# The closing of an expert layer: the residual of all groups but the last beside the last products, two norms together, and gathers paced in two parts

## The chip, the cores and the metric

The kernel runs on one core of one Trainium2 chip. The metric is the device time of one execution in microseconds, the median of the runs shown. The engines are named as in the profile: PE is TensorE (its matrix products, with PEld the loading of weights), DVE is VectorE, ACT is ScalarE, POOL is GpSimd, SP is SyncE, whose queue issues most of the transfers. A line such as L1323 is a line of the kernel before.

## The reference

One layer over 1024 latent tokens of width 1024 (and 256 context tokens): a mixer (a Mamba-2 head group and a convolution group, one output projection), then a retrieval layer over 16384 single-neuron experts, then a norm. The change touches only the retrieval layer's end and its order:

```
s = einsum(q, sub_keys); sv, si = top_k(s, 16)              # per token, 8 heads, two halves of the key
best, flat = top_k(sv0[:, None] + sv1[None, :], 16)         # the choice: 8 x 16 = 128 experts a token
experts, gates = i1 * 128 + i2, softmax(best)
act = gelu(einsum("pd,ped->pe", x, u_tab[experts]))
y   = einsum("pe,ped->pd", gates * act, v_tab[experts])
x   = x + mod5 * y
return rms_norm(x, final_norm_w)                            # x * rsqrt(mean(x*x) + eps) * w
```

## The kernel before

**Two ways to the same sum.** The 1024 tokens are eight blocks of 128. The first ND = 5 blocks are computed densely: the 16384 experts are cut into 128 tiles, called experts here, of 128 neurons; for each of them PE multiplies all 640 tokens by the tile's u (In), ACT takes the Gelu, DVE weighs it with a matrix of gates that is zero where a token has not chosen the neuron, and PE multiplies the result by the tile's v (Out). The other three blocks are gathered: for each token and each of its 128 choices one row of u and later one row of v is fetched by an indirect transfer of POOL (128 rows of 1024 numbers, one to a partition), and one instruction of DVE uses it: L1311 multiplies with the token and sums (a u step), L1323 multiplies by the weight and adds to `ac` (a v step). A block has 128 u steps and 128 v steps, so there are 768 row steps.

**Products in three.** Every fp32 product is made as three in a reduced format, of high and low parts. ACT makes the high part (`hi_lo`, L60; L984 for u; L1412 for the weighed activations), DVE the low one by a subtraction (L61, L988, L1416). So each In and Out needs an instruction of ACT and then one of DVE before PE can multiply.

**The order of the expert loop** is written out by hand. GE = 8 experts are a group, and there are 16 groups. `seq` holds 8 Ins, then for each group 8 Outs of the first half of the columns (512), one In of the next group, 8 Outs of the second half, 7 Ins. In one item: begin the splits, loads and gates that are due some items ahead; weigh the In before; the item's products (`mm`); then `advance`; then the low half of the In before, and the Gelu. The five PSUM tiles `pv` (one a block) collect the 8 Outs of a half, and `Out.sum` (L1457) adds them to `acc`, which is a part of h2T, after each half of each group. The last half of the last group is not run in the loop: its eight Outs are `closing`.

**advance** is what puts other work beside the products. An In calls it with (2, 18), an Out with (1, 11): so many pieces of the last choice (block 7's top-k on DVE, with parts on POOL; 100 pieces in all), and so many units on `units[0]`. For the units, it runs steps of the generator `gathered()`: one row step each, 768 of them, and ten more with which the last block is closed (`finish`, L1258 to L1274: its residual, its norm and its output). Experts 0 to 2 call no advance. While the choice runs there are NGB = 5 buffers for gathered rows; when it has ended, its memory is freed and NMORE = 2 more are opened. What is left of the steps after the loop runs in one go.

**The end before.** In the last eight Outs of the loop the memory of the Ins is given back (at the second of them, `far == 1`), and rw (the gate row, broadcast), final_norm_w and the five x1 tiles are loaded through SP's queue; the splits of the closing Outs are begun two more ahead with every Out, up to all eight. Behind the loop, block by block: `Close.mm` multiplies the block's 24 closing products into a PSUM tile `pf` (three buffers); `residual(0)` computes acc * rw + x1 on the first 512 columns of the next block, and ACT its squares' sum; `post` adds pf to the second 512 columns, does their residual, sums the squares, takes the inverse root (`rsqrt`, L95 to L101, small instructions of DVE around one Sqrt of ACT), scales the 1024 columns (L1494) and issues the block's output.

Of the kernel before, what the change touches and what calls it, by code (L numbers as in the profile page):

```python
# [8 lines left out]
F32 = mybir.dt.float32  # L9
# [4 lines left out]
AF = mybir.ActivationFunctionType  # L14
OP = mybir.AluOpType
# [3 lines left out]
P = 128  # L19
D = 1024  # L20
KD = D // P
T = 1024
NT = T // P
# [10 lines left out]
NEXP = 16384  # L34
# [3 lines left out]
ND = 5  # L38
# [2 lines left out]
NS = 7  # L41
NGB, NMORE = 5, 2
IN_US, OUT_US = 18, 11
NU, NV = 3, 3
GE = 8

# [26 lines left out]
def layer_kernel(ctx, tc, A, dbg=None):  # L73
    nc = tc.nc
# [98 lines left out]
    with ExitStack() as st:  # L173
# [12 lines left out]
        for j in range(8):  # L186
# [5 lines left out]
            c = (j + 4) % 8 * 256  # L192
# [179 lines left out]
    with ExitStack() as st:  # L372
# [126 lines left out]
        for n, c in enumerate(order):  # L499
# [13 lines left out]
            elif c >= 16 and c < 20:  # L513
                i = c - 16
# [262 lines left out]
    with ExitStack() as st:  # L777
# [63 lines left out]
        def residual(z, half, x1, p):  # L841
            cs = slice(half * 512, half * 512 + 512)
            nc.vector.tensor_tensor(x1[:, cs], p, gater[:, cs], op=OP.mult)
            nc.vector.tensor_tensor(x1[:, cs], x1[:, cs], B[z][0][:, cs], op=OP.add)
# [399 lines left out]
    with ExitStack() as st:  # L1244
# [85 lines left out]
        more, self_end = [], object()  # L1330
        steps = gathered()
        next(steps)
        units = [0, 0]

        SE = {}

# [20 lines left out]
        def advance(n, us):  # L1357

            for _ in range(n):
                if not more and next(choice, self_end) is self_end:  # L1360

                    last_choice.close()
                    more.append(st.enter_context(tc.tile_pool(name="more", bufs=NMORE, reuse_waits="tile")))
            units[0] += us
            while units[1] * (NEXP // P * (IN_US + 2 * OUT_US) - 3 * IN_US) < units[0] * ((NT - ND) * 2 * P + 20):
                next(steps, None)
                units[1] += 1

        W = {}
        NG = NEXP // P // GE  # L1370
# [47 lines left out]
        class Out:  # L1418
# [28 lines left out]
                advance(1, OUT_US)  # L1447

            def sum(self):
                if self.i < GE - 1:  # L1450
                    return
                for t in range(ND):
                    a = acc[:, t, self.cs]
                    if self.g == 0:
                        nc.scalar.activation(a, Out.pv[t], AF.Copy)
                    else:
                        nc.vector.tensor_tensor(a, a, Out.pv[t], op=OP.add)  # L1457
# [4 lines left out]
        class Close:  # L1462
# [6 lines left out]
                self.x = tail.tile([P, D], F32, name="x1", bufs=ND)  # L1469
                nc.sync.dma_start(self.x, x1_dram[self.t * P:(self.t + 1) * P, :])  # L1470

            def residual(self, half):
                cs = slice(half * 512, half * 512 + 512)
                a = self.a[:, cs]
                nc.vector.tensor_tensor(a, a, rw[:, cs], op=OP.mult)
                nc.vector.tensor_tensor(a, a, self.x[:, cs], op=OP.add)
                nc.scalar.activation(self.x[:, cs], a, AF.Square, accum_out=sf[:, self.t, half:half + 1])

            def mm(self, outs):
                self.pv = psF.tile([P, 512], F32, name="pf")  # L1480
# [3 lines left out]
                    for j, (x, y) in enumerate(((wl, o.vh), (wh, o.vl), (wh, o.vh))):  # L1484
                        nc.tensor.matmul(self.pv, x[:, sl], y, start=o.i == 0 and j == 0, stop=o.i == GE - 1 and j == 2)

            def post(self):
                t, a = self.t, self.a
                nc.vector.tensor_tensor(a[:, 512:], a[:, 512:], self.pv, op=OP.add)
                self.residual(1)  # L1490
                s2, r = sf[:, t, 2:3], sf[:, t, 3:4]
                nc.vector.tensor_tensor(s2, sf[:, t, 0:1], sf[:, t, 1:2], op=OP.add)
                rsqrt(r, s2, 1.0 / D, 1)
                nc.vector.scalar_tensor_tensor(a, a, r, spare_w, op0=OP.mult, op1=OP.mult)  # L1494
                nc.sync.dma_start(A["out"][t * P:(t + 1) * P, :], a)

        seq = [In(i) for i in range(GE)]
        for g in range(NG):
# [29 lines left out]
        for n, x in enumerate(seq[:-GE]):  # L1528
            far = 0
            if len(seq) - n <= 2 * GE:  # L1530
                far = x.i
                if far == 1:

                    late.close()
                    tail = late.enter_context(tc.tile_pool(name="tail", bufs=GE, side="right", reuse_waits="tile"))
                    psF = late.enter_context(tc.tile_pool(name="psF", bufs=3, space=PSUM, side="right", reuse_waits="tile"))
                    rw = tail.tile([P, D], F32, name="rw", bufs=1)
                    nc.sync.dma_start(rw, row_dram[0].partition_broadcast(P))
                    nc.sync.dma_start(spare_w, A["final_norm_w"].partition_broadcast(P))
                    sf = tail.tile([P, ND, 4], F32, name="sf", bufs=1)  # L1540
                    ends = [Close(t) for t in range(ND)]
                    for c in ends:
                        c.load()
            begin(In, "split", 2)
            begin(Out, "split", 2 + far)
            begin(Out, "load", NV + 2 + far)
            before = seq[n - 1] if n and isinstance(seq[n - 1], In) else None
            if before:
                before.weigh()
            passed[type(x)] += 1  # L1550
            begin(In, "gate", 2)
            begin(In, "lower", 1)
            begin(In, "load", NU + 1)
            x.mm()
            if before:
                before.low()
            x.post()
        for _ in steps:
            pass
        dbg("idx", idx)  # L1560
        dbg("gates", gates)
        begin(Out, "split", GE)
        ends[0].residual(0)
        for c in ends:
            c.mm(closing)
            if c.t + 1 < ND:
                ends[c.t + 1].residual(0)
            c.post()
    late.close()
    sel.close()  # L1570

# [59 lines left out]
```

## Time and profile before

| | |
|---|---|
| median of 3 runs | 3053.84 us (3052.66 to 3054.78) |
| the profiled execution: time, span | 3052.06 us, 3050.3 us |
| PE busy | 2836.3 us, 93% |
| DVE busy | 2570.6 us, 84% |
| ACT busy | 1060.9 us, 35% |
| POOL busy | 1326.0 us, 43% |
| mean granted clock of PE | 0.968 |

The span runs from the first to the last instruction; the time of the execution holds 1.8 us more around it. The busy shares are means over stages that differ: a stage is judged by what waits in it. A wait stands in brackets behind an instruction as the idle time of its engine before it, and what ended it.

### The profile page before, as it was taken

To read this page: it belongs to the slowest core of one execution; us is meant where nothing else is said; L and a number is where in the kernel's file an instruction comes from. 1 tells how busy PE (TensorE), PEld (TensorE's weight loads), DVE (VectorE), ACT (ScalarE), POOL (GpSimd) and SP (SyncE) were. 2 spreads that over 40 slices of the span, in tenths; PEclk is the share of its full clock that TensorE was granted. 3 is DMA by queue.
4 is the path that set the end of the run, shared out by engine and by line. 5 is a ranking of instruction groups with operands and counts; after the bars stand their busy time and mean duration, and the time that the engine had idled before them with its cause. 6 is when DMAs were issued, how large, how long until landed. Compare 5 with 4: busy or idle time off the path is not lost.

```text
span 3050.3 us, 41960 instructions
## 1 busy us (share of the span) xinstructions
PE 2836.3 (93%) x15129; PEld 2391.2 (78%) x15129; DVE 2570.6 (84%) x5084; ACT 1060.9 (35%) x2026; POOL 1326.0 (43%) x1043
## 2 busy tenths in 40 slices
PE   7999899998888876999999999999999999999996
PEld 3777698764555556898888998998998898998995
DVE  4898756659999999889989998888998888888886
ACT  3224333333667664332222222222222322322222
POOL 0212343420000002666566656566666566666650
PEclk8999899999999987999999999999999999999998
DMA  6211256250221235888889999998998998999993
GB/s 214 61 36 42 86 165 213 77 189 15 118 107 63 111 125 192 308 312 301 311 297 361 324 346 343 326 340 320 337 344 317 334 357 318 336 342 318 328 326 119
DMA packets 334545, 722.68 MB, mean 237 GB/s; under 512 B 24560, under 2 KB 167168, under 8 KB 333056
## 3 DMA queue, kind: packets, MB, share of 16 engines
q0 software_dynamic: 112176, 408.47, 37.1%
q1 hardware_dynamic: 222160, 311.53, 29.5%
q8 instruction: 119, 1.95, 0.2%
q14 instruction: 90, 0.74, 0.1%
HBM read 658.56 MB, written 61.35 MB: 236 GB/s over the span
## 4 chain that ended last, share of the span: by engine, by line
PE 58%; DVE 27%; issue 5%; DMA 5%; POOL 3%; ACT 2%; SPq 0%; DVEq 0%; POOLq 0%; ACTq 0%
PE pa L996 22%; PE pv L1444 8%; PE pv L1445 8%; PE pv L1443 8%; PE pa L68 4%; DVE o L1219 3%; DVE cfm L413 2%; DVE oh L1091 2%; DVE ob L1211 2%; POOL gr L1286 2%; DVE oh L1089 2%; DVE gr L1311 1%; DVE ef L1077 1%; PE pq L953 1%; PE po L68 1%
## 5 line engine op out<-in xcount | busy, mean ns | idle before, releaser
L1286 POOL DMA_INDIRECT gr<-in_peer_v_dram,idx x384 | 546.8, 1424 | 309.3 <-DVE h2T L1323 209.7
L1286 POOL DMA_INDIRECT gr<-in_peer_u_dram,idx x384 | 524.1, 1365 | 361.4 <-DVE gr L1311 249.2
L1444 PE MATMUL pv<-vl,wh 128*128 128x512 f32 x1240 | 495.5, 400 | 19.5 <-DVE vl L61 17.3
L1323 DVE SCALAR_TENSOR_TENSOR h2T<-gr,wv,h2T 128x1024 f32<-128x1024 f32 x381 | 488.5, 1282 | 13.6 <-DMA gr<-in_peer_v_dram,idx 6.0
L1443 PE MATMUL pv<-vh,wl 128*128 128x512 f32 x1240 | 493.4, 398 | 1.5 <-ACT vh L60 1.4
L1445 PE MATMUL pv<-vh,wh 128*128 128x512 f32 x1240 | 493.6, 398 | 0.0
L1311 DVE SCALAR_TENSOR_TENSOR gr<-gr,h2T 128x1024 f32<-128x1024 f32 x384 | 455.5, 1220 | 23.5 <-DMA gr<-in_peer_u_dram,idx 23.3
L60 ACT ACTIVATE vh<-v 128x512 fp32r<-128x512 f32 x256 | 161.5, 632 | 656.1 <-PE pv L1445 616.7
L996 PE MATMUL pa<-hh,ul 128*128 128x320 f32 x2000 | 335.0, 310 | 3.2 <-DVE ul L988 3.2
L996 PE MATMUL pa<-hh,uh 128*128 128x320 f32 x2000 | 334.6, 309 | 0.0
L996 PE MATMUL pa<-hl,uh 128*128 128x320 f32 x2000 | 334.0, 309 | 0.3 <-ACT ga L1406 0.3
L996 PEld LDWEIGHTS pa<-hl,uh 128*128 128x128 f32 x2000 | 304.8, 188 | 3.3 <-ACT ga L1406 0.6
L996 PEld LDWEIGHTS pa<-hh,ul 128*128 128x128 f32 x2000 | 304.2, 188 | 3.7 <-DVE ul L988 3.7
L996 PEld LDWEIGHTS pa<-hh,uh 128*128 128x128 f32 x2000 | 304.4, 188 | 0.0
L1444 PEld LDWEIGHTS pv<-vl,wh 128*128 128x128 f32 x1240 | 235.0, 190 | 80.0 <-DVE vl L61 22.8
L1406 ACT ACTIVATE ga<-pa 128x320 f32<-128x320 f32 x252 | 109.2, 436 | 525.2 <-PE pa L996 507.1
L1443 PEld LDWEIGHTS pv<-vh,wl 128*128 128x128 f32 x1240 | 235.1, 190 | 57.8 <-ACT vh L60 2.4
L61 DVE TENSOR_TENSOR vl<-v,vh 128x512 fp32r<-128x512 f32 x256 | 176.4, 690 | 122.5 <-ACT vh L60 114.9
L1445 PEld LDWEIGHTS pv<-vh,wh 128*128 128x128 f32 x1240 | 235.3, 190 | 56.1
L1197 PEld LDWEIGHTS pg<-o,o 128*128 128x128 f32 x1280 | 174.1, 207 | 128.2 <-ACT o L1214 109.2
L1197 PE MATMUL pg<-o,o 128*128 128x128 f32 x1280 | 188.0, 297 | 75.7 <-ACT o L1214 67.3
L1214 ACT ACTIVATE o<-ob,tr 128x128 f32<-128x128 bf16 x640 | 209.4, 399 | 96.4 <-DVE ob L1211 94.4
(344 smaller groups left out, 4241.5 us busy)
## 6 DMA issues: line engine op xcount, KB each, us to landing
v<-in_peer_v_dram SPq DMA_DIRECT2D x256, 256.0 KB
u<-in_peer_ut_dram SPq DMA_DIRECT2D x87, 512.0 KB
g_dram<-stg SPq DMA_DIRECT2D x10, 4096.0 KB
gm<-g_dram SPq DMA_DIRECT2D x64, 640.0 KB
h2T<-in_peer_ut_dram SPq DMA_DIRECT2D x41, 512.0 KB
ld<-in_ada_w_dram SPq DMA_DIRECT2D x24, 512.0 KB
w<-in_w_in_t_dram SPq DMA_DIRECT2D x21, 512.0 KB
raw<-in_ada_w_dram SPq DMA_DIRECT2D x8, 1024.0 KB
```

The lines of the kernel that those rows point to most:

```text
L60: nc.scalar.activation(hi, src, AF.Copy)
L61: (eng or nc.vector).tensor_tensor(lo, src, hi.bitcast(F32), op=OP.subtract)
L68: nc.tensor.matmul(out, a(k)[i], b(k)[j], start=start and t == 0 and k == 0, stop=stop and t == 2 and k == n - 1)
L996: nc.tensor.matmul(pa[half], x[:, k], y[:, k, half * TH:half * TH + TH], start=t == 0 and k == 0, stop=t == 2 and k == KD - 1)
L1197: nc.tensor.matmul(pg[:, j], o2[:, j], o1[:, j], start=True, stop=True)
L1214: nc.scalar.activation(o2[:, j], ob[:, :, j], AF.Copy, scale=tr[:, 1, t4 * 4 + j:t4 * 4 + j + 1])
L1286: nc.gpsimd.indirect_dma_start(out=g, out_offset=None, in_=A[t], in_offset=bass.IndirectOffsetOnAxis(ap=idx[:, b, e:e + 1], axis=0))
L1311: nc.vector.scalar_tensor_tensor(g, g, 1.0, h2, op0=OP.mult, op1=OP.mult, accum_out=act[:, e:e + 1])
L1323: nc.vector.scalar_tensor_tensor(ac, g, wv[:, e:e + 1], ac, op0=OP.mult, op1=OP.add)
L1443: nc.tensor.matmul(Out.pv[t], wl[:, sl], self.vh, start=i == 0, stop=False)
L1444: nc.tensor.matmul(Out.pv[t], wh[:, sl], self.vl, start=False, stop=False)
L1445: nc.tensor.matmul(Out.pv[t], wh[:, sl], self.vh, start=False, stop=i == GE - 1)
```

## The change

- `advance` runs its steps at two paces. Until the choice is done, a unit is worth 0.85 x 782 / 4918 steps (before: 788 / 5066); from then on, what is left of 782 is spread over what is left to unit 4918, that is LEAD = 60 units before the loop's end at unit 4978. So all steps, the closing of the last block too, are issued within the loop.
- `Out.sum` is left out for the last group. In the last Outs of the loop (from `far == 4` on, one block each) and behind the loop (block 4), `residual` computes a * rw + x1 on all 1024 columns, of the sums of all groups but the last.
- Behind the loop, `add(0, pv)` for the five blocks: x = pv * rw, a += x, and ACT the squares' sum, on the first half; the second half likewise from pf after each block's closing products.
- `norm` takes the inverse roots of blocks 0 and 1 together, and 2 and 3; then `post` scales. Block 3 is scaled after block 4's add, block 4 alone, in two halves with an output each.

```diff
+LEAD = 60
@@ advance
-            units[0] += us
-            while units[1] * (NEXP // P * (IN_US + 2 * OUT_US) - 3 * IN_US) < units[0] * ((NT - ND) * 2 * P + 20):
+            end, num = NEXP // P * (IN_US + 2 * OUT_US) - 3 * IN_US - GE * OUT_US - LEAD, (NT - ND) * 2 * P + 14
+            units[1] += us * (0.85 * num / end if not more else (num - units[2]) / max(end - units[0], us))
+            units[0] += us
+            while units[2] < min(units[1], num):
                 next(steps, None)
-                units[1] += 1
+                units[2] += 1
@@ Out.sum
-                if self.i < GE - 1:
+                if self.i < GE - 1 or self.g == NG - 1:
                     return
@@ Close
-            def residual(self, half):
+            def residual(self):
+                nc.vector.tensor_tensor(self.a, self.a, rw, op=OP.mult)
+                nc.vector.tensor_tensor(self.a, self.a, self.x, op=OP.add)
+
+            def add(self, half, pv):
                 cs = slice(half * 512, half * 512 + 512)
-                a = self.a[:, cs]
-                nc.vector.tensor_tensor(a, a, rw[:, cs], op=OP.mult)
-                nc.vector.tensor_tensor(a, a, self.x[:, cs], op=OP.add)
-                nc.scalar.activation(self.x[:, cs], a, AF.Square, accum_out=sf[:, self.t, half:half + 1])
+                a, x = self.a[:, cs], self.x[:, cs]
+                nc.vector.tensor_tensor(x, pv, rw[:, cs], op=OP.mult)
+                nc.vector.tensor_tensor(a, a, x, op=OP.add)
+                nc.scalar.activation(x, a, AF.Square, accum_out=sf[:, half, self.t:self.t + 1])
@@ Close.post
-            def post(self):
-                t, a = self.t, self.a
-                nc.vector.tensor_tensor(a[:, 512:], a[:, 512:], self.pv, op=OP.add)
-                self.residual(1)
-                s2, r = sf[:, t, 2:3], sf[:, t, 3:4]
-                nc.vector.tensor_tensor(s2, sf[:, t, 0:1], sf[:, t, 1:2], op=OP.add)
-                rsqrt(r, s2, 1.0 / D, 1)
-                nc.vector.scalar_tensor_tensor(a, a, r, spare_w, op0=OP.mult, op1=OP.mult)
-                nc.sync.dma_start(A["out"][t * P:(t + 1) * P, :], a)
+            @staticmethod
+            def norm(t, n):
+                ts = slice(t, t + n)
+                nc.vector.tensor_tensor(sf[:, 2, ts], sf[:, 0, ts], sf[:, 1, ts], op=OP.add)
+                rsqrt(sf[:, 3, ts], sf[:, 2, ts], 1.0 / D, n)
+
+            def post(self, parts=1):
+                t, a, w = self.t, self.a, D // parts
+                for cs in (slice(i * w, i * w + w) for i in range(parts)):
+                    nc.vector.scalar_tensor_tensor(a[:, cs], a[:, cs], sf[:, 3, t:t + 1], spare_w[:, cs], op0=OP.mult, op1=OP.mult)
+                    nc.sync.dma_start(A["out"][t * P:(t + 1) * P, cs], a[:, cs])
@@ the loop, and behind it
             x.post()
+            if far > 3:
+                ends[far - 4].residual()
         for _ in steps:
             pass
+        ends[ND - 1].residual()
         begin(Out, "split", GE)
-        ends[0].residual(0)
         for c in ends:
+            c.add(0, Out.pv[c.t])
+        for c in ends[:ND - 1]:
             c.mm(closing)
-            if c.t + 1 < ND:
-                ends[c.t + 1].residual(0)
-            c.post()
+            c.add(1, c.pv)
+            if c.t % 2:
+                Close.norm(c.t - 1, 2)
+                ends[c.t - 1].post()
+                if c.t == 1:
+                    c.post()
+        c = ends[ND - 1]
+        c.mm(closing)
+        c.add(1, c.pv)
+        ends[ND - 2].post()
+        Close.norm(c.t, 1)
+        c.post(2)
```

## Rows read from the trace of the kernel before

**Rows 1.** The page, busy time of each engine and its share.
```profile
PE 2836.3 (93%) x15129; PEld 2391.2 (78%) x15129; DVE 2570.6 (84%) x5084; ACT 1060.9 (35%) x2026; POOL 1326.0 (43%) x1043
```

**Rows 2.** The chain that ended last: start, length, what (expert 32's In first).
```profile
1641.39 7.04 PE pa L996 x48
...
1753.71 7.04 PE pa L996 x48
...
1868.64 7.04 PE pa L996 x48
```

**Rows 3.** Windows: stretch, length, busy time of PE to POOL, clock, DMA share, GB/s.
```profile
1204.40:1641.39 436.99, 416.52 (x2256) 372.06 (x2255) 390.71 (x782) 130.37 (x210) 268.83 (x223) 0.97 0.89 310
...
1610.00:1722.32 112.32, 112.23 (x623) 101.01 (x622) 102.36 (x103) 30.98 (x50) 73.34 (x51) 1.00 0.97 350
...
2171.60:2283.92 112.32, 112.32 (x626) 101.44 (x626) 100.73 (x101) 30.27 (x49) 71.57 (x51) 1.00 0.93 333
```

**Rows 4.** The same windows, L1323 alone: DVE's busy time and count.
```profile
1610.00:1722.32 112.32, 65.15 (x51) 1.00 0.97 350
...
2171.60:2283.92 112.32, 64.10 (x50) 1.00 0.93 333
```

**Rows 5.** Waits from 1600 to 2960: who for whom, total us, times, longest.
```profile
DVE vl L61 <- ACT vh L60: 91.1, 122, 1.7
```

**Rows 6.** Timeline of PE, the start of expert 3's In.
```profile
1207.41 1.34 PE L996 MATMUL pa<-hl,uh 128*128 128x320 f32 x8
```

**Rows 7.** Waits from 1204.4 to 1641.39.
```profile
DVE gr L1311 <- DMA gr<-in_peer_u_dram,idx: 22.1, 12, 5.7
...
PE pv L1444 <- DVE vl L61: 15.3, 8, 3.8
```

**Rows 8.** Timeline of PE: the loop's last eight Outs start; the last product.
```profile
2966.19 0.39 PE L1443 MATMUL pv<-vh,wl 128*128 128x512 f32 x1
...
3027.07 0.39 PE L1485 MATMUL pf<-vh,wh 128*128 128x512 f32 x1
```

**Rows 9.** Timeline of DVE in the last 90 us.
```profile
2960.56 3.92 DVE L1323 SCALAR_TENSOR_TENSOR h2T<-gr,wv,h2T 128x1024 f32<-128x1024 f32 x3
...
2988.05 0.69 DVE L61 TENSOR_TENSOR vl<-v,vh 128x512 fp32r<-128x512 f32 x1 [2.80 <-ACT vh L60]
...
2991.18 1.89 DVE L61 TENSOR_TENSOR vl<-v,vh 128x512 fp32r<-128x512 f32 x3
...
3003.78 1.22 DVE L1263 TENSOR_TENSOR h2T<-h2T,gr 128x1024 f32<-128x1024 f32 x1
3005.04 1.23 DVE L1266 TENSOR_TENSOR h2T<-h2T,gr 128x1024 f32<-128x1024 f32 x1
...
3011.16 0.68 DVE L1475 TENSOR_TENSOR h2T<-h2T,rw 128x512 f32<-128x512 f32 x1
...
3019.53 0.69 DVE L1475 TENSOR_TENSOR h2T<-h2T,rw 128x512 f32<-128x512 f32 x1
...
3020.86 0.68 DVE L1489 TENSOR_TENSOR h2T<-h2T,pf 128x512 f32<-128x512 f32 x1
...
3023.79 0.16 DVE L1492 TENSOR_TENSOR sf<-sf 128x1 f32<-128x1 f32 x1 [0.79 <-ACT x L1477]
...
3025.38 1.28 DVE L1494 SCALAR_TENSOR_TENSOR h2T<-h2T,sf 128x1024 f32<-128x1024 f32 x1
...
3045.16 1.29 DVE L1494 SCALAR_TENSOR_TENSOR h2T<-h2T,sf 128x1024 f32<-128x1024 f32 x1
```

**Rows 10.** Timeline of SP's queue: rw is issued.
```profile
2959.34 0.33 SPq L1538 DMA_DIRECT2D rw<-row_dram  x1
```

**Rows 11.** Timeline of ACT in the last 90 us.
```profile
2981.40 0.63 ACT L60 ACTIVATE vh<-v 128x512 fp32r<-128x512 f32 x1 [3.87 <-DMA v<-in_peer_v_dram]
...
3007.47 1.28 ACT L96 ACT_TABLE_LOAD   x1
3008.76 0.20 ACT L96 ACTIVATE rs<-rs 128x1 f32<-128x1 f32 x1
```

More of the change, by code (lines that the diff above doesn't have):

```diff
@@ L1332, in layer_kernel @@
         next(steps)
-        units = [0, 0]
+        units = [0, 0.0, 0]
         SE = {}
@@ L1539, in layer_kernel @@
                     nc.sync.dma_start(spare_w, A["final_norm_w"].partition_broadcast(P))
-                    sf = tail.tile([P, ND, 4], F32, name="sf", bufs=1)
+                    sf = tail.tile([P, 4, ND], F32, name="sf", bufs=1)
                     ends = [Close(t) for t in range(ND)]
```

## The prediction

> **What bounds the kernel now.** The page first: TensorE (PE) is busy 93% of a span of 3050.3 us, VectorE (DVE) 84% [rows 1]. That is an average over stages, so the change is read in three stretches: the expert loop beside the last choice, the loop behind it, and the end.
>
> *Behind the choice* the chain of waits is nothing but products: one group of eight experts starts 112.32 us after the one before, and a group in which a block of tokens is finished takes 114.93 us [rows 2]; there are two of these. PE is busy 112.32 of 112.32 us. DVE has 100.73 us of work there, 50 row steps among it [rows 3, 4], and what it waits for is ScalarE (ACT), 91.1 us in 122 waits [rows 5]: it is ahead of PE. PE's own rate bounds this stretch.
>
> *Beside the choice* it is not so. The In of expert 3 starts at 1207.41 [rows 6]. At 7.04 us for an In and 3.50 for an Out ((112.32 - 8 x 7.04) / 16) the In of expert 32, 29 Ins and 56 Outs later, would start after 400.2 us, at 1607.6. It starts at 1641.39 [rows 2]: 33.8 us are lost. PE is busy 416.52 of 437 us, so it stands still for 20.5, 15.3 of them in eight waits for lower halves of v [rows 3, 7]; and the granted clock is 0.97, between the levels of 1.2 and 2.4 GHz, which is 3% of 437 us, some 13. That is all. DVE is the cause: busy 390.71 of 437 us [rows 3], and idle 22.1 us, in 12 waits, for gathered u rows that have not landed [rows 7]. Every row step is a DVE instruction in order before the next lower half, so a late row holds PE.
>
> *At the end* PE's last product starts at 3027.07 [rows 8], the last instruction of DVE ends at 3046.45 [rows 9] and the span at 3050.3. From the lower half at 2988.05 on, DVE is what ends last.
>
> **The pace.** Before: 3 x 256 + 20 = 788 steps over 128 x 40 - 54 = 5066 units, 0.1556 a unit. The choice has 100 pieces, two to an In and one to an Out, and ends in the In of expert 29 at 996 units: 155 steps are behind it by then. After: 0.85 x 782 / 4918 = 0.1352 (768 + 14 steps; 5066 - 88 - 60 units), so 135 steps; from there 647 steps in 3922 units, 0.165. A group has 320 units: 49.8 steps before, 43.3 beside the choice and 52.8 behind it after.
>
> Twenty steps leave the stretch beside the choice. Those that leave are all v steps (the 128 u steps stay), 1.30 us each, three in 3.92 [rows 9]: 26 us of DVE. They can give PE no more than the 33.8 us lost. DVE's work there falls to about 365 us in a stretch that PE alone would do in 403: the saturated engine becomes one with 9% of room, as it has behind the choice. But the waits for rows are not all of the pace: there are only five buffers until the choice is done, POOL computes pieces of the choice between its gathers, and Ins and Outs issue their steps in bursts. A buffered row is now consumed 112.32 / 43.3 - 112.32 / 49.8 = 0.34 us later than the one before it was; over four buffered rows a landing has 1.4 us more, against a mean wait of 22.1 / 12 = 1.8 us and a longest of 5.7. So the typical wait nearly goes and the long ones stay, shortened. The floor of the gain is 0 (all waits stay and PE's stalls with them), the ceiling 33.8; I take 60% of it, 20, nearer the ceiling because both causes, backlog and late rows, shrink, and fewer stalls also mean less time at the lower clock.
>
> The same twenty steps, and the ten that close the last block, come behind the choice. A group of v steps then holds 100.73 + 3 x 1.28 = 104.6 us of DVE for 112.32 of PE: hidden behind the products. Each step gathers 512 KB: three more make 333 GB/s into about 347. The group from 1610 has 51 steps at 350 GB/s and PE at 112.23 us [rows 3, 4], so both have been borne. At the two block ends, which cost 2.6 us each now (114.93 - 112.32), the wait for the norm's weights behind more gathers may grow by half a microsecond or one each. I take +1.5 for the stretch; bounds 0, and 6 if these waits double.
>
> **The last block's closing** (L1258 to L1274) moves before the last Outs. Its last row step falls about 14 / 0.165 = 85 units before unit 4918, in the In of expert 124, its Sqrt and output into that of 127. It leaves the end: 3003.78 to 3011.16, 7.4 us [rows 9]. What it passes: its output transfer stands on SP's queue now ahead of rw, final_norm_w, the five x1 tiles and the last v tiles; SP waits there for DVE until about 2967, where today rw went out at 2959.34 [rows 10]. The v tile for which ACT waits 3.87 us today, to 2981.40 [rows 11], is needed by PE five Outs after 2966.19 [rows 8], at 2983.7, less some 0.65 us for each half to be cut: 1.0 us of room, against 1.5 MB more behind 2967 (the output, rw, final_norm_w) and some gathers fewer. I charge 0.8 us; without a shift it is 0, with all 1.5 MB at 340 GB/s 4.4 less the room, 3.4.
>
> **The end on DVE, from 2988.05.** That lower half waits for ACT, and ACT for PE, so nothing moved earlier starts before it: the five residuals stand behind it in order. What DVE then does:
> - nine lower halves (the last of the half before and the eight to close), three in 1.89 us: 5.7
> - five residuals of 1024 columns: 1.26 from start to start for the first part (as the finished block's at 3003.78 and 3005.04), 1.20 for the second: 2.46 each, 12.3. The last v tiles' reloads, three buffers wide, run under them; if they land later than DVE has the residuals' work for, DVE waits for them as it does now
> - ten pairs of multiply and add on 512 columns: 3019.53 to 3020.86, 1.33 each, 13.3
> - norm of blocks 0 and 1: from the end of an add (0.79 before 3023.79) to the scaling at 3025.38, 2.4, and 0.9 for the table load (below): 3.3. Norm of 2 and 3: 2.4. I take two columns to cost what one does: such an instruction is 0.16 us long, nearly all of it not the column
> - scaling blocks 0, 1, 2: 1.20 each, 3.6
> - block 3's scaling (1.2) under the last block's square, which ends 0.8 after its add; then the small chain 3023.79 to 3025.38, 1.6; two halves of the last scaling 1.3
>
> Sum 44.7: DVE ends at 3032.75 instead of 3046.45. PE does not hold it: after the stall for the last halves, block 3's and 4's products wait for PSUM buffers that the first multiplies free, at about 3013.4 and then 5.6 us a block, so block 4 is done at 3024.9, and DVE asks for it at 3027.3. From the last scaling's end to the span's end it was 3.85 us with 512 KB; the last piece is now 256 KB: 3.3, between 2.8 and 3.85. The span's end comes at 3036.0 + 0.8: 13.5 us are saved, between 10 (late v tiles) and 16.
>
> The table load runs from 3007.47 for 1.28 us and the square root follows at 3008.76 [rows 11]. Today there is one such load at the end. After, the closing's Sqrt comes before the Gelu of expert 127, so tables go to Sqrt, to Gelu and back to Sqrt; the last lies on the path, 1.28 less some 0.4 that the square root waits there anyway for two small instructions of DVE (0.16 each and the handing over), 0.9. The Trainium skill ("ScalarE: Activation LUTs", What ACT_TABLE_LOAD costs) speaks against mixing sets so: it gives a switch 1.28 us for the load and 1.38 for a drain. The trace agrees on the load and shows no drain between load and square root; by the page the sum would be 1.4 us longer.
>
> **Sum.** -20 (choice) + 1.5 (behind it) - 13.5 (end) = -32. The profiled execution took 3052.06, its span 3050.3; the median of the runs is 1.8 above that. Median 3053.84 - 32 = 3022.
>
> **Rivals.**
> 1. *The choice stretch keeps its stalls* (late rows, not pace, are the cause; total DVE work is the same): gain there 0 to 12. For it: PE's long stalls follow DVE waits for rows of up to 5.7 us. Against: DVE is 89% busy there as well. With 4: -4 + 1.5 - 13.5, 3038.
> 2. *The stretch is cured*: gain 28 to 33.8, 3009 to 3014. For it: behind the choice, DVE at 90% costs PE nothing. Against: five buffers instead of seven.
> 3. *Slower: the transfers become the bound behind the choice.* If no more than the 333 GB/s of the usual group could be had, 53 steps would take 347/333 x 112.32 = 117 us, +4.7 a group over twelve groups, +56: 3054 - 33.5 + 56 = 3076. It decides from 2.8 us a group, below about 339 GB/s. Against: 350 GB/s with PE full.
> 4. *The pace changes nothing and the end is held by late v tiles* (10 saved), with 6 lost behind the choice: 3050, no change.
>
> Chances: forecast (3014 to 3031) 0.56, rival 1 0.20, rival 2 0.14, rival 3 0.05 (half of it past the point), rival 4 0.05. The range from 3008 to 3040 leaves out the lower end of rival 2, the upper end of rival 1, and rivals 3 and 4, together no more than 2 in 10; the forecast's own range is 3014 to 3031. A run of this kernel tells about 0.2% (6 us) from no change; slower 0.03, same 0.05, faster 0.92.
>
> **What would show it.** Expert 32's In starts near 1621 instead of 1641 (from 1207), fewer PE stalls on lower halves and a clock nearer 1.00 there; groups of 112.3 us behind it with 53 steps and no DVE wait for rows; no closing of the last token block among the last products; from the lower half that starts at 2988.05 now to the end of the span 48 us instead of 62. Wrong would make it: waits of POOL's gathers that do not fall; groups over 113 us; splits of the last v tiles that wait for transfers behind the residuals; a clock of 1.2 GHz in the last products, which would bring block 4 to DVE some 3 us late.

## The result and the profile after

The kernel after takes 3016.91 us (median of 4 runs, 3015.12 to 3022.14), the kernel before 3053.25 in the same set: a ratio of 0.9886, 95% interval 0.9873 to 0.9900, or 36 us. 3022 was forecast. The profiled execution has a span of 3015.6 us against 3050.3, 34.7 less.

The span falls into four pieces by PE's own instructions: up to the first Out of the loop, from there to the In of expert 32 (the choice lies in this piece), from there to the loop's last eight Outs, and from there to the end. Two rows of PE's timeline after mark the last piece, the start of the last eight Outs and the last product; before, these stood at 2966.19 and 3027.07 [rows 8]:

```profile
2946.08 0.39 PE L1447 MATMUL pv<-vh,wl 128*128 128x512 f32 x1
...
3003.91 0.40 PE L1495 MATMUL pf<-vh,wh 128*128 128x512 f32 x1
```

Expert 32's In starts at 1616.05 in the chain of waits after (1641.39 in [rows 2]). The chain of the kernel after, from there:

```profile
1616.05 7.04 PE pa L997 x48
...
1728.37 7.04 PE pa L997 x48
1763.41 49.28 PE pa L997 x336
...
1880.77 49.28 PE pa L997 x336
```

Groups still follow each other in 112.32 us (1728.37 - 1616.05); the group in which a block is closed takes 117.36 (1880.77 - 1763.41), where it took 114.93.

Windows of the kernel after (columns as in [rows 3]): the stretch beside the choice, a group of v steps, the group with the second block end; then, for the group of v steps, L1324 alone:

```profile
1205.00:1616.05 411.05, 406.92 (x2256) 367.15 (x2255) 367.21 (x763) 131.74 (x210) 239.32 (x204) 0.99 0.87 305
...
2182.68:2295.01 112.33, 112.33 (x627) 101.44 (x626) 102.91 (x103) 30.39 (x48) 74.27 (x52) 1.00 0.97 346
2295.01:2412.65 117.64, 114.64 (x626) 102.33 (x626) 106.92 (x127) 32.93 (x52) 75.11 (x56) 0.99 0.93 339
```
```profile
2182.68:2295.01 112.33, 66.68 (x52) 1.00 0.97 346
```

DVE's work beside the choice fell from 390.71 to 367.21 us, PE's standing still from 20.5 to 4.1 (411.05 - 406.92), and the clock rose from 0.97 to 0.99. Waits after, from 1204 to 1625, for [rows 7]:

```profile
DVE gr L1312 <- DMA gr<-in_peer_u_dram,idx: 14.8, 9, 5.7
...
PE pv L1448 <- DVE vl L62: 4.1, 2, 2.1
```

DVE still waits 14.8 of the 22.1 us for rows, the longest still 5.7, and yet PE waits for lower halves 4.1 instead of 15.3. That is the first sign of what the experiments show: what costs PE is less the late rows than that DVE has no time to make them good.

The end on the timeline of DVE after, for [rows 9]:

```profile
2945.37 1.28 DVE L1274 SCALAR_TENSOR_TENSOR h2T<-h2T,sf,gr 128x1024 f32<-128x1024 f32 x1
...
2967.94 1.90 DVE L62 TENSOR_TENSOR vl<-v,vh 128x512 fp32r<-128x512 f32 x3 [2.80 <-ACT vh L61]
2969.76 1.22 DVE L1478 TENSOR_TENSOR h2T<-h2T,rw 128x1024 f32<-128x1024 f32 x1
...
2985.46 0.68 DVE L1485 TENSOR_TENSOR x<-pv,rw 128x512 f32<-128x512 f32 x1
...
2995.63 0.16 DVE L1501 TENSOR_TENSOR sf<-sf 128x2 f32<-128x2 f32 x1 [0.79 <-ACT x L1487]
...
2998.14 2.48 DVE L1507 SCALAR_TENSOR_TENSOR h2T<-h2T,sf 128x1024 f32<-128x1024 f32 x2
...
3010.99 1.42 DVE L1507 SCALAR_TENSOR_TENSOR h2T<-h2T,sf 128x512 f32<-128x512 f32 x2
```

From the lower half that waits for PE (2967.94; 2988.05 before) DVE works to 3012.41 with no wait but those for ACT in the norms: 44.5 us instead of 58.4. Then 3.2 us to the end of the span. The token block's closing (L1274) is over before the last Outs.

All runs by these pieces (one profiled execution each, us). The first piece is left out: it ended between 1241.9 and 1249.6, and the part of it that the edits reach, from expert 3's In to the first Out, took 35.2 us in every run.

| kernel | first Out to In 32 | In 32 to last Outs | last Outs to end | median, us | ratio to before (95%) |
|---|---|---|---|---|---|
| before | 398.6 | 1325.0 | 84.1 | 3053.25 | |
| after | 372.7 | 1330.2 | 69.5 | 3016.91 | 0.9886 (0.9873 to 0.9900) |
| pace_only | 377.0 | 1328.8 | 75.8 | 3029.7 | 0.9921 (0.9894 to 0.9948) |
| end_only | 396.6 | 1326.2 | 76.7 | 3046.33 | 0.9977 (0.9962 to 0.9991) |
| one_pace | 395.2 | 1325.3 | 71.6 | 3044.54 | 0.9971 (0.9957 to 0.9986) |
| pace_070 | 365.1 | 1335.9 | 71.3 | 3021.92 | 0.9901 (0.9872 to 0.9929) |
| short_steps | 368.9 | 1326.6 | 84.7 | one run, 3024.75 | |
| no_finish | 370.9 | 1319.8 | 70.2 | one run, 3008.58 | |
| norm_on_sp | 374.8 | 1326.0 | 69.4 | one run, 3013.87 | |
| early_res | 373.3 | 1327.9 | 69.0 | one run, 3019.18 | |
| after_again | 370.6 | 1327.6 | 69.5 | 3018.95 | 0.9885 (0.9870 to 0.9900) |
| best_070 | 365.1 | 1329.7 | 74.8 | 3015.36 | 0.9870 (0.9855 to 0.9885) |
| best_075 | 365.0 | 1332.6 | 75.1 | 3018.04 | 0.9887 (0.9870 to 0.9904) |
| final_070 | 365.1 | 1327.7 | 70.5 | 3011.83 | 0.9857 (0.9833 to 0.9880) |

A piece of one execution has a spread of its own. The six executions that run the choice at the pace of after with all of DVE's work (after, pace_only, no_finish, norm_on_sp, early_res, after_again) took 370.6 to 377.0 us in the first column; the four of them that leave the block ends alone (after, pace_only, early_res, after_again) took 1327.6 to 1330.2 in the second. Differences smaller than these are not read. The line numbers of the kernels built on after lie a little higher than those of before: L62 is the lower half of L61, L1312 and L1324 are the row steps of L1311 and L1323, L1448 is the product of L1444.

### The profile page after: what moved, and what is told of

Its sections match the earlier page's. It is cut to its first block, busy times and chain, and to the rows that moved or that the text cites. A ratio compares the mean times of both kernels' runs of the same rounds, so it can differ in the third digit from the quotient of the medians.

```text
span 3015.6 us, 41945 instructions
## 1 busy us (share of the span) xinstructions
PE 2832.4 (94%) x15129; PEld 2390.9 (79%) x15129; DVE 2572.1 (85%) x5071; ACT 1065.1 (35%) x2026; POOL 1336.4 (44%) x1043
## 4 chain that ended last, share of the span: by engine, by line
PE 66%; DVE 26%; DMA 2%; ACT 2%; issue 2%; POOL 1%; SPq 0%; DVEq 0%; POOLq 0%; ACTq 0%
PE pa L997 27%; PE pv L1448 9%; PE pv L1449 9%; PE pv L1447 9%; DVE o L1220 3%; DVE cfm L414 3%; PE pa L69 3%; DVE oh L1092 2%; DVE ob L1212 2%; DVE oh L1090 2%; DVE ef L1078 1%; PE pq L954 1%; PE po L69 1%; PE pk L362 1%; PE pc L335 1%
## 5 line engine op out<-in xcount | busy, mean ns | idle before, releaser
L1287 POOL DMA_INDIRECT gr<-in_peer_u_dram,idx x384 | 534.9, 1393 | 346.6 <-DVE gr L1312 237.8
L1448 PE MATMUL pv<-vl,wh 128*128 128x512 f32 x1240 | 493.8, 398 | 9.0 <-DVE vl L62 8.9
L1324 DVE SCALAR_TENSOR_TENSOR h2T<-gr,wv,h2T 128x1024 f32<-128x1024 f32 x381 | 488.6, 1282 | 7.8 <-DMA gr<-in_peer_v_dram,idx 0.3
L1312 DVE SCALAR_TENSOR_TENSOR gr<-gr,h2T 128x1024 f32<-128x1024 f32 x384 | 455.1, 1219 | 16.6 <-DMA gr<-in_peer_u_dram,idx 16.4
L61 ACT ACTIVATE vh<-v 128x512 fp32r<-128x512 f32 x256 | 161.6, 632 | 645.1 <-PE pv L1449 617.4
L1448 PEld LDWEIGHTS pv<-vl,wh 128*128 128x128 f32 x1240 | 234.6, 189 | 66.8 <-DVE vl L62 11.7
L62 DVE TENSOR_TENSOR vl<-v,vh 128x512 fp32r<-128x512 f32 x256 | 176.4, 690 | 111.8 <-ACT vh L61 108.5
```

The source lines that it names most:

```text
L61: nc.scalar.activation(hi, src, AF.Copy)
L62: (eng or nc.vector).tensor_tensor(lo, src, hi.bitcast(F32), op=OP.subtract)
L1287: nc.gpsimd.indirect_dma_start(out=g, out_offset=None, in_=A[t], in_offset=bass.IndirectOffsetOnAxis(ap=idx[:, b, e:e + 1], axis=0))
L1312: nc.vector.scalar_tensor_tensor(g, g, 1.0, h2, op0=OP.mult, op1=OP.mult, accum_out=act[:, e:e + 1])
L1324: nc.vector.scalar_tensor_tensor(ac, g, wv[:, e:e + 1], ac, op0=OP.mult, op1=OP.add)
L1448: nc.tensor.matmul(Out.pv[t], wh[:, sl], self.vl, start=False, stop=False)
```

## The experiments

**The two halves of the change, each alone.**

```diff
# pace_only: the kernel before with
-            while units[1] * (NEXP // P * (IN_US + 2 * OUT_US) - 3 * IN_US) < units[0] * ((NT - ND) * 2 * P + 20):
+            units[1] += us * (0.85 * num / end if not more else (num - units[2]) / max(end - units[0], us))
+            while units[2] < min(units[1], num):
# the line that sets end and num, and the counters, are left out here
# end_only: the kernel after with the old lines there
```

> The kernel before with the new advance alone (two paces, all steps within the loop); the end as before. If twenty row steps fewer beside the choice give what the two traces show there (the In of expert 32 comes 408 us after that of expert 3 instead of 434), and the closing of the last token block (7.4 us) and its last row steps leave the end, the time is 3053 - 26 + 5 - 9 = 3023 us. If the gain beside the choice comes with the new end in some way, it stays above 3040.

> The kernel after with the old advance: only the new end. The closing of the last token block then stands in DVE's order among the residuals and the last adds again, with its last row steps: some 7.4 + 4 us of the 14.6 that the end gave come back, so 3053 - 3 to 5 = 3049 us, and the stretch beside the choice is 434 us as before. If the rewritten residual is what shortens the end whatever the pace, the time is 3053 - 14 = 3039.

Measured 3029.7 and 3046.33 (both on a chip where before took 3053.85). Beside the choice the pace alone gives 21.6 us and the new end alone 2.0, so that gain is the pace's. Each alone takes 8.3 and 7.4 us from the end, 15.7 together where the two do 14.6: half of the end's gain is the rewritten residual, half the closing of the last token block that is out of the way. Both expected times were missed. pace_only came 6.7 us above 3023, as its choice gave 21.6 us where after's trace had 26. For end_only 3049 was expected; of the 11.4 us that were to come back at the end 7.2 did (76.7 - 69.5).

**One pace, but early.** `0.85 * num` becomes `1.0 * num`.

> The kernel after with a factor of 1.0 for 0.85: beside the choice 0.159 steps a unit, as many as before (158 for 155), but still all steps 60 units ahead of the loop's end. If the relief of DVE beside the choice is the cause, the stretch from expert 3 to expert 32 is back at 434 to 440 us and the time near 3042. If ending the steps early is the cause, the time stays near 3017.

395.2 us beside the choice, some 3.5 us less than before with three steps more, and 71.6 at the end. From expert 3's In it is 430.3 us, a little under the 434 to 440 expected; the median of 3044.54 is near the 3042 expected. Ending the steps early gives the end its gain and the choice nearly none: the factor does it.

**A slower pace beside the choice.** `0.85 * num` becomes `0.70 * num`.

> The kernel after with a factor of 0.70: 110 steps beside the choice instead of 135, 55 a group behind it. Backlog of DVE as the cause: the stretch falls from 408 to 401-403 us, PE's own 400.2 being the floor; late rows behind POOL's pieces of the choice as the cause of what is left: it stays at 406-408. Behind it the two block ends cost 6 to 7 us each instead of 5, or, if transfers become the bound there at some 356 GB/s, each group of gathered v rows takes over 113 us and the time is above 3025. Else 3012 to 3018.

Windows of pace_070, beside the choice and a later group of v steps, then L1324 alone:

```profile
1205.00:1608.35 403.35, 403.35 (x2255) 365.27 (x2254) 339.84 (x739) 132.46 (x210) 194.27 (x181) 1.00 0.83 280
2175.88:2288.20 112.32, 112.32 (x627) 101.49 (x626) 106.00 (x106) 30.41 (x48) 77.24 (x55) 1.00 0.97 351
```
```profile
2175.88:2288.20 112.32, 70.52 (x55) 1.00 0.97 351
```

PE is busy all the 403.35 us, at full clock: 365.1 us from the first Out to In 32 is PE's own time, and the 33.8 us that the prediction counted as lost are all to be had. Nothing is left for POOL's pieces of the choice to explain. Behind the choice 55 steps and 351 GB/s still fit into 112.32 us: the transfers do not become the bound. The gain is eaten elsewhere: the second piece is 10.9 us longer than before, all of it at the two block ends, whose groups take 118.3 and 122.4 us, 5.9 and 10.1 more than 112.32 where 6 to 7 were expected. The total is no better than with 0.85, and 3021.92 lies above the 3012 to 3018 expected.

**DVE's work or late rows?** The kernel before at its old pace, with DVE's row steps cut to 512 columns while the choice runs, and everything else left.

```diff
+                    w = D if more else D // 2
-                    nc.vector.scalar_tensor_tensor(g, g, 1.0, h2, op0=OP.mult, op1=OP.mult, accum_out=act[:, e:e + 1])
+                    nc.vector.scalar_tensor_tensor(g[:, :w], g[:, :w], 1.0, h2[:, :w], op0=OP.mult, op1=OP.mult, accum_out=act[:, e:e + 1])
# and the same for the v step
```

> The kernel before at its old pace, but beside the choice DVE's row steps use only 512 of the 1024 columns (part of the sum is left out); the gathers, their number, bytes and times of issue stay. DVE's work as the cause: some 155 steps shorter by 0.5 us each, more than the 26 us that the new pace took away, so the stretch from the first Out to expert 32's In falls from 398.6 us to PE's own 365 to 370. Late rows as the cause, whatever DVE's work: it stays above 385.

Waits of short_steps, 1205 to 1611.8:

```profile
DVE gr L1312 <- DMA gr<-in_peer_u_dram,idx: 28.8, 26, 4.5
DVE h2T L1325 <- DMA gr<-in_peer_v_dram,idx: 12.2, 9, 5.1
...
PE pv L1446 <- DVE vl L61: 3.2, 2, 1.8
```

368.9 us. DVE now waits 41 us for rows, more than the 28 of before (22.1 for rows of u and 6.0 for rows of v), and PE stands still for 3.2. So rows may be late as they are; what PE loses is set by how much work DVE has between them. It is this run that decides against the first rival. pace_070 alone would not, because at its pace the waits for rows shrink too, to 5.8 us in two waits.

**The block ends.** Without the closing of the first two gathered blocks:

```diff
-                done = finish(ND + b, ac)
+                done = finish(ND + b, ac) if b + 1 == NT - ND else iter([nc.sync.dma_start(A["out"][(ND + b) * P:(ND + b + 1) * P, :], ac)])
```

> The kernel after without the closing of the first two gathered blocks (their sums are put out as they are, without residual and norm). If the closing is what makes the two block ends long (117.4 and 117.6 us for a group instead of 112.3), all groups behind the choice take 112.3 us and the stretch from expert 32 to the last Outs is 1320 us instead of 1330. If it is the change from v steps to u steps or the load of the next tokens, it stays at 1328 to 1330.

Chain of no_finish over the first block end, and over the second:

```profile
1764.32 49.28 PE pa L997 x336
...
1876.64 49.28 PE pa L997 x336
...
2325.92 49.28 PE pa L997 x336
2438.24 49.28 PE pa L997 x336
```

Both groups take 112.32 us, and the piece 1319.8: the closing makes the block ends long, nothing else does, and the tight pace costs nothing outside them. The other half of the question is what in the closing does it. The load of final_norm_w moves to SP's queue:

```diff
-            nc.gpsimd.dma_start(rw, A["final_norm_w"].partition_broadcast(P))
+            nc.sync.dma_start(rw, A["final_norm_w"].partition_broadcast(P))
```

> The kernel after with the closing's load of final_norm_w issued by SP's queue instead of POOL's (one word). If that load, queued behind up to six gathers of 512 KB, holds the buffer and so DVE and the next gathers, the two block ends lose most of their 5 us: 1322 to 1325 us from expert 32 to the last Outs. If the two tiles that the closing takes from the seven are the cause, it stays at 1328 to 1330; and SP's waiting for DVE there may hold loads of u, which would lengthen a group.

1326.0 us, 4.2 less than the execution of after in the table, and all of it at the second end, as the chain of norm_on_sp shows:

```profile
1764.27 49.28 PE pa L997 x336
...
1881.70 49.28 PE pa L997 x336
...
2330.98 49.28 PE pa L997 x336
...
2444.32 49.28 PE pa L997 x336
```

The first end is unchanged (117.43), the second falls from 117.64 to 113.34. Two things fall together there, and only one of them is the queue's. In after DVE waited at the second end for final_norm_w (2.07 us, first row) and PE then for late lower halves (3.0 us, next two rows); in norm_on_sp DVE does not wait for final_norm_w, and PE waits 0.36 us (last row). DVE, then PE of the kernel after at its second end; PE of norm_on_sp there:

```profile
2400.99 1.29 DVE L1274 SCALAR_TENSOR_TENSOR h2T<-h2T,sf,gr 128x1024 f32<-128x1024 f32 x1 [2.07 <-DMA gr<-in_final_norm_w_dram]
```
```profile
2397.82 0.50 PE L1448 MATMUL pv<-vl,wh 128*128 128x512 f32 x1 [0.46 <-DVE vl L62]
2404.08 0.67 PE L1448 MATMUL pv<-vl,wh 128*128 128x512 f32 x1 [2.50 <-DVE vl L62]
```
```profile
2402.21 0.50 PE L1448 MATMUL pv<-vl,wh 128*128 128x512 f32 x1 [0.36 <-DVE vl L62]
```

The other thing is the clock: in after the group of the second end has a granted clock of 0.99 and its products take 114.64 us (windows above), in norm_on_sp 1.00 and 112.87. That comes and goes without any edit of the closing: early_res has the wait for final_norm_w (1.86 us) and PE's wait behind it (2.28), but a clock of 1.00, and its second end takes 115.2 us. So of the 4.3 us about 2 are the queue's; the 1322 to 1325 us expected were not reached.

At the first end DVE did not wait for final_norm_w in after either, and PE waits all the same. PE of the kernel after there, then the lower half for which it waits the second time:

```profile
1855.93 0.50 PE L1447 MATMUL pv<-vh,wl 128*128 128x512 f32 x1 [1.20 <-ACT vh L61]
1858.27 0.80 PE L1448 MATMUL pv<-vl,wh 128*128 128x512 f32 x1 [1.84 <-DVE vl L62]
```
```profile
1857.53 0.69 DVE L62 TENSOR_TENSOR vl<-v,vh 128x512 fp32r<-128x512 f32 x1
```

No experiment takes the first end apart, but the trace speaks for the closing's own instructions and against the two buffers of the seven that it holds. If it were the buffers, rows would come late and DVE would wait for them. From 1838.43 to 1861.11 DVE waits for no row; its only waits there over 0.2 us are 0.59 and 0.27 us, for ACT. ACT's order is held by the closing's square root from 1846.11 to 1850.70: a table load of 1.28 us, a wait of 1.80 for DVE, the root, and a load of 1.28 back for the Gelu.

**The end's order.** The residuals two Outs earlier:

```diff
-            if far > 3:
-                ends[far - 4].residual()
+            if 1 < far < ND + 2:
+                ends[far - 2].residual()
# without the residual behind the loop
```

> The kernel after with the residuals two Outs earlier (far from 2 instead of 4), so that one stands before DVE's lower half that waits for PE, the other four behind it. If DVE's order behind that lower half sets the end, as the sum of the prediction has it, the end (last Outs to the end of the span, 69.5 us) is shorter by one residual, 2.4 us: 67.1. If the v tiles' reloads or PE set it, it stays at 69 to 70.

69.0, not 67.1, so the second of the two outcomes came. DVE did get 2.5 us ahead: its first add stands 36.9 us behind the last Outs' start (2985.26 - 2948.40) instead of 39.4. But the others now stand before the last splits, PE waits for these twice (in after once, 1.55 us), and DVE later waits for PE. PE, then DVE of early_res:

```profile
2981.20 0.50 PE L1495 MATMUL pf<-vl,wh 128*128 128x512 f32 x1 [1.61 <-DVE vl L62]
2984.80 0.51 PE L1495 MATMUL pf<-vl,wh 128*128 128x512 f32 x1 [1.93 <-DVE vl L62]
```
```profile
3003.07 0.69 DVE L1485 TENSOR_TENSOR x<-pf,rw 128x512 f32<-128x512 f32 x1 [1.32 <-PE pf L1495]
```

The end of the kernel after is bound by DVE, but PE has less than 3 us of room: its last product starts at 3003.91 and DVE asks for the sum at 3006.89.

**Towards a better version.** These are the kernel after once more, and two that put together the lower factor, final_norm_w by SP's queue, and the residuals of blocks 1 to 4 on POOL:

```diff
+                eng = nc.vector if self.t == 0 else nc.gpsimd
-                nc.vector.tensor_tensor(self.a, self.a, rw, op=OP.mult)
-                nc.vector.tensor_tensor(self.a, self.a, self.x, op=OP.add)
+                eng.tensor_tensor(self.a, self.a, rw, op=OP.mult)
+                eng.tensor_tensor(self.a, self.a, self.x, op=OP.add)
```

> The kernel after once more, on one chip with the two that follow: 3017 us, a ratio of 0.9886 to the kernel before.

> A factor of 0.70, final_norm_w by SP's queue, and the residuals from far = 2 on, that of block 0 on DVE and the other four on POOL. By the sum: 365 us from the first Out to expert 32's In, 1323 to 1330 behind it (the factor alone gave 1336, the queue took 4 from 1330), and an end of 65 to 66 us, because four residuals of 2.46 leave DVE's order and PE's own products (56 us from the last Outs, then 9.3) become the bound: 3000 to 3008. If POOL's instructions share DVE's way to memory, or are slower than 2.5 us each, the end stays at 69.

> The same with a factor of 0.75: 366 to 368 us beside the choice, 1322 to 1328 behind it, the same end: within 4 us of the factor 0.70, either way.

The kernel after came out at 0.9885 in this set, near its 0.9886 above. The choice and the stretch behind it came as expected for 0.70 (365.1 and 1329.7); for 0.75 the stretch behind it took 1332.6, above the 1322 to 1328 expected. The end is 74.8 and 75.1, longer than without POOL, so both times lie above 3000 to 3008. Timelines of DVE and of POOL in best_070:

```profile
2962.00 3.41 DVE L1479 TENSOR_TENSOR h2T<-h2T,rw 128x1024 f32<-128x1024 f32 x1
2965.45 3.27 DVE L1480 TENSOR_TENSOR h2T<-h2T,x 128x1024 f32<-128x1024 f32 x1
2968.64 6.80 DVE L62 TENSOR_TENSOR vl<-v,vh 128x512 fp32r<-128x512 f32 x4
```
```profile
2956.71 2.39 POOL L1479 TENSOR_TENSOR h2T<-h2T,rw 128x1024 f32<-128x1024 f32 x1
...
2964.41 3.22 POOL L1480 TENSOR_TENSOR h2T<-h2T,x 128x1024 f32<-128x1024 f32 x1
```

The same instruction that takes DVE 1.22 us alone takes 3.41 beside POOL's, a lower half 1.7 instead of 0.63, and POOL's own grows from 2.39 to 3.22. PE pays for the late lower halves: the longest of its waits for them there is 5.62 us, at 2971.52. So POOL's work was taken back:

```diff
# final_070: 0.70, final_norm_w by SP, and
-            if far > 3:
-                ends[far - 4].residual()
+            if far == 2 or far > 3:
+                ends[max(far - 3, 0)].residual()
# without the residual behind the loop
```

> A factor of 0.70, final_norm_w by SP's queue, and all residuals on DVE: block 0's at far = 2, blocks 1 to 4 at far = 4 to 7. Beside the choice 365 us, behind it 1328 to 1331, both as the same two edits gave with POOL's residuals. The end: one residual of 2.46 us leaves DVE's order behind the lower half that waits for PE, and unlike the shift of all five it puts none before the last splits, so PE is not delayed: 67 us instead of 69.5. Together some 10 us under the kernel after: 3005 to 3009, a ratio of 0.985. If the splits are delayed all the same, the end stays at 69.

3011.83 us, 0.9857 (0.9833 to 0.9880): the lowest ratio of all the kernels that compute the whole result, some 9 us under the kernel after by the ratios (0.9886 and 0.9885), but the intervals overlap, so that it is faster than the kernel after is not shown. The first two pieces came as expected. The end is 70.5, not 67, and DVE's first add stands 39.4 us behind the last Outs' start (2977.43 - 2938.05), just as in after: the residual that left DVE's order brought nothing. With 0.70 the closing's last instruction stands 1.4 us behind the start of the last Outs (2939.46 to 2938.05) instead of 0.7 before it, SP's loads wait for it, and a v tile is late, for which PE pays at once (first two rows). PE waits again for the last splits (third row; 1.55 us in after), and DVE at the end twice for PE (0.46 and 0.47). PE's timeline of final_070:

```profile
2956.72 0.50 PE L1447 MATMUL pv<-vh,wl 128*128 128x512 f32 x1 [1.01 <-ACT vh L61]
2957.45 0.51 PE L1448 MATMUL pv<-vl,wh 128*128 128x512 f32 x1 [0.23 <-DVE vl L62]
...
2974.57 0.50 PE L1495 MATMUL pf<-vl,wh 128*128 128x512 f32 x1 [1.96 <-DVE vl L62]
```

## Why the prediction was right

- **What bounds each stretch** was read rightly: PE's rate behind the choice, DVE beside it and at the end. The first two were shown: no_finish has groups of 112.32 us at the new pace, and short_steps frees DVE and the choice's loss is gone. At the end the rows agree, as DVE works through with no wait but for ACT; early_res shows that PE stands close behind.
- **The total** came nearer than its terms: -36 for -32. By the pieces the choice gave 5.9 us more than forecast and the end 1.1 more, and the stretch behind the choice took 3.7 more than forecast; that these go against each other is luck.
- **The choice.** -20 was forecast, -25.9 came, of a possible 33.8. The main cause, DVE's backlog, was right, the term too small: 60% was taken because the late rows were held to be a second cause, with the typical wait nearly gone and the long ones shortened. The waits hardly changed (nine of 1.6 us in the mean for twelve of 1.8, the longest still 5.7), but a DVE with room absorbs most of them; 77% came (64% to 83% over the five other executions at this pace), and 99% with a factor of 0.70. With one pace (one_pace) nearly all of the loss stayed, so it is the twenty steps. One sign of being wrong that the prediction named, waits of POOL's gathers that do not fall, did come and was no good sign: POOL waited 148.8 us for DVE to free a buffer, before 134.8, and PE's stalls fell all the same.
- **Behind the choice.** +1.5 was forecast, within 0 to 6; +5.2 came, and +2.6 in a second execution of the same kernel (1327.6 - 1325.0). The place was right, the two block ends, the size too small. The cause that was named, the wait for the norm's weights, holds for one of the two: before, DVE waited for them at both ends (1.55 and 1.41 us), after only at the second (2.07). Windows of PE over the first block end, for the kernel before, for after, and for after_again, which is the same kernel:

```profile
1788.75:1903.68 114.93, 112.84 (x626) 1.00 0.95 344
```

```profile
1763.41:1880.77 117.36, 114.31 (x627) 0.99 0.95 347
```

```profile
1766.09:1881.96 115.87, 112.83 (x626) 1.00 0.95 347
```

  PE stood still for 2.1 us (114.93 - 112.84) and now for some 3.0 (117.36 - 114.31 and 115.87 - 112.83). In after the same products also take 114.31 instead of 112.84 us, at a granted clock of 0.99; in after_again, with the same waits of PE (1.19 and 1.84 us), the clock stays at 1.00 and they take 112.83. That part comes and goes between executions. The clock was not counted there, though it was beside the choice.
- **The end.** -13.5 was forecast, -14.6 came. DVE's sum from the lower half that waits for PE was 44.7, measured 44.5; the last transfer 3.3 and 3.2. The 0.8 us charged for SP's queue were too much in after: the tile that was late is there 15.75 us after the last Outs' start (2961.83 - 2946.08), where it was there after 15.21, and PE had the room for it. In final_070 the same queue did cost PE 1.2.
- **The table load.** There are three now, as said: one for the closing's square root, one back for the Gelu, one in the end. ACT after:

```profile
2942.87 1.28 ACT L97 ACT_TABLE_LOAD   x1
2944.17 0.20 ACT L97 ACTIVATE rs<-rs 128x1 f32<-128x1 f32 x1
2944.39 1.28 ACT L1410 ACT_TABLE_LOAD   x1
2945.68 0.44 ACT L1410 ACTIVATE ga<-pa 128x320 f32<-128x320 f32 x1
...
2995.61 1.28 ACT L97 ACT_TABLE_LOAD   x1
2996.91 0.20 ACT L97 ACTIVATE rs<-rs 128x2 f32<-128x2 f32 x1
```

  The first norm took 3.31 us on the path (add's end at 2994.83 to 2998.14), 3.3 was forecast. The Trainium skill ("ScalarE: Activation LUTs", What ACT_TABLE_LOAD costs) adds a drain of 1.38 us to each switch; here the next function follows 1.3 us after the load's start in each case, so its load time holds and its drain does not show.
- **The rivals.** The first fell with short_steps; the second is what pace_070 does beside the choice and after nearly does (the low end of its times is 3008 by the prediction's own terms, not 3009); the third fell with 55 steps at 351 GB/s in 112.32 us; the fourth did not occur.

## What to carry to other kernels

Here an engine that was 89% busy (390.71 of 437 us) and waited another 6% for data was the bound, though no single wait looked like it. Try to take work from such an engine: here the waits for data that remained nearly stopped costing, because it could catch up. Work that was moved out of the saturated stretch was free where another engine bounded, except at that stretch's own tight places, so look for these first; here they were the two block ends in 1330 us, and they took back 5 of 26 us, and at a lower pace 11 of 33. For an end in which one engine works in order, count its instructions from the last outside wait: here that gave the end to 0.2 us in 44. The count holds for the order counted: when one residual was moved ahead in early_res and final_070, the 2.4 us came back as waits on another engine.

## What was not expected of the hardware

- A stall of PE of some 3 us can cost more than itself. After 2.50 us of waiting at the second block end of after the granted clock of the group was 0.99 instead of 1.00, and of 5.3 us lost there PE stood still for 3.0. It need not: at the first end PE's waits were the same in after and in after_again, and the clock of the group 0.99 in one and 1.00 in the other. What decides it is not shown.
- DVE and POOL working at once, each on 1024 columns from two tiles, slowed each other: DVE 1.22 to 3.41 us, POOL 2.39 to 3.22. The Trainium skill ("SBUF — State Buffer", SBUF: two separate sides) tells of a pair of ports that DVE's instructions with two inputs share with POOL's reads, one blocking the other for a whole instruction; the trace agrees that both lose, and the 3.41 us stay under the 1.22 + 2.39 of one behind the other.
